# A hybrid mLSTM and delta-rule layer on one core: transposes, UL copies, sums and filler pieces of the delta rule placed differently

## The chip, the cores and the metric

The kernel runs on one core of a Trainium2 chip. The metric is the device time of one execution in microseconds. Several executions were timed, and the time of a kernel is their median. A profile is of one single execution, with a time of its own. Engines are named as in the profile: PE is TensorE (matmuls; PEld its weight loads), DVE is VectorE, ACT is ScalarE, POOL is GpSimd, SP is the engine whose queue issues most loads from memory.

## The reference

One layer, 256 tokens, model width 2048, fp32. Two recurrent branches read the same normalised input; each is projected, gated and merged, then a SwiGLU feed-forward part (FFN) follows.

```python
mod = c_act @ ada_w + ada_b                      # six vectors of 2048: shift, scale, gate, twice
h = rms_norm(x, norm_mix_w) * (1 + scale_m) + shift_m
proj = h @ w_in
(a_q, a_k, a_v, a_o, a_i, a_f, b_qkv, b_z, b_beta, b_a, merge) = jnp.split(proj, IN_SPLITS, axis=-1)
...
h_a = bidirectional(mlstm_chunkwise, (q_a, k_a, v_a), ...)          # 4 heads
y_a = (sigmoid(a_o) * rms_norm(h_a, mlstm_norm_w)) @ w_branch_a
qkv = silu(centred_depthwise_conv(b_qkv, gdn_conv_w))
...
o_b = bidirectional(gated_delta_chunkwise, (q_b, k_b, v_b), ...)    # 16 heads of 128
y_b = (rms_norm(o_b, gdn_norm_w) * silu(b_z)) @ w_branch_b
x = x + gate_m * ((g_a * y_a + g_b * y_b) @ w_out)
hf = rms_norm(x, norm_ffn_w) * (1 + scale_f) + shift_f
x = x + gate_f * ((silu(gt) * up) @ w_down)      # gt, up = split(hf @ w_gate_up)
```

The gated delta rule works in chunks of 64 tokens, forward and backward. Each chunk needs the inverse of a 64 x 64 unit triangular matrix:

```python
a_mat = eye(CHUNK) + betac[..., :, None] * einsum('nbhid,nbhjd->nbhij', kc, kc) * decay_strict
t_mat = triangular_solve(a_mat, eye(CHUNK), left_side=True, lower=True, unit_diagonal=True)
```

## The kernel before

Every projection is a matmul in which both sides are split into a high and a low part, three products each. The weights come from memory in chunks of 1 MB into `raw` (three buffers, loads issued on the SP queue). ScalarE copies half a chunk into `wh`, VectorE makes `wl` as the difference, and TensorE multiplies `wh` by the high part of the activation, `wh` by the low part, and `wl` by the high part. `wh` and `wl` have three buffers each. Half a chunk is one piece: twelve matmuls with 512 columns in `tjob` (lines 165, 166, 181 to 183), or 24 with 256 columns in `fjob` and in the jobs of the delta rule's own projections (lines 141, 142, 145 to 147; their tiles carry the letter b and the head, as in acc_b).

Jobs that nobody waits for soon are kept as a list of pieces, `fills`: `fill(n)` issues the next n of them, in the order z (the output gate of a group's heads), v, mb, o, a, ma and so on. They are put between the steps of the serial parts, so that TensorE has work while those steps wait for other engines. The total number of pieces is fixed; whatever is not used early is issued at the end of the stage by `fill(1000)`.

A second list, `background`, holds the sums of the modulation vectors (`ada_part` 2, 3 and 4, 17 items each): a 1 MB load into a `raw` buffer, then one VectorE instruction of line 110, which multiplies it by the conditioning row and accumulates. `pump()` is called at the end of every job or chunk and issues one sum at each `every[0]`-th call; at 0 there are none. `sums(n)` issues n at once.

The sixteen heads of the delta rule are worked in four groups of four, each group in two pairs:

- `gdn_phase1` of a head: convolution taps on VectorE (line 263, tile cv), SiLU on ScalarE (line 264: kq, vf), transposes of vf into vps (line 496), norms, the products ks (line 524), masks, and copies of blocks into cc on ScalarE (lines 553, 556). Blocks go to memory and come back packed as `uu` (line 548).
- `gdn_invert` of a group: a serial loop on VectorE over `uu`, 30 steps (lines 576 and below), that inverts the 32 x 32 diagonal blocks. Its first instruction, the memset of line 571, needs uu to have arrived. Between stretches of the loop one piece is issued.
- `gdn_blocks` of a group: the inverted blocks come back as `cg`; from it the tiles R, X (line 610, ScalarE) and UL (line 615, eight copies of 32 x 256 on ScalarE, four for i = 0 and four for i = 1).
- `gdn_phase2` of a pair, nine steps: p1 to p4 build the inverse from the blocks (lines 630 to 666, with mask products pt on VectorE), then pa, pb, pc (lines 676 to 688, with copies z on ScalarE, lines 680 and 681), po, a norm, and last the transposes px (line 713) and per head a copy `obt` on ScalarE (line 715) that goes to memory.

The driver runs the nine steps of a pair and puts pieces between them (the tuples `after` and `last`); the pieces are the projections of the next pair of heads, taken from `stream`, then filler. After the two pairs of a group it puts the next group's z job in front of the filler and runs the next inversion. Most of the heavier instructions pass through `order(...)`, and the program's scheduler decides the final place of the instructions in each engine's queue.

Behind the delta rule comes the mLSTM stage: loads of the branch results (`o_load`), loads in `mlstm(h)`, pieces in front of and between them. Then the branch projections yb and ya, the output projection with `wo` in four jobs (o0 to o3, each of four chunks, two pieces a chunk) that end in `residual` on VectorE, and the FFN.

Of the kernel before, what the change touches and what calls it, by code (L numbers as in the profile page):

```python
# [11 lines left out]
AF = mybir.ActivationFunctionType  # L12
# [40 lines left out]
def hybrid_block(ctx: ExitStack, tc: tile.TileContext, xr, nfr, crow, pk_d, cst_d, ada2, ada4, win0, winb, wint, wba, wbb, wo, wgu, wd, out, dbg=None):  # L53
    nc = tc.nc
    V, S, G, PE = nc.vector, nc.scalar, nc.gpsimd, nc.tensor
# [12 lines left out]
    def big(p, dt, name):  # L68
        return p.tile([P, KB, T], dt, tag="b16", name=name)

    def order(ins, yes=True):

        return tc.keep_in_program_order(ins) if yes else ins
# [43 lines left out]
    count, every = [0], [0]  # L117

    def sums(n=1):

        while n and background:
            if next(background[0], None):
                n -= 1
            else:
                background.pop(0)

    def pump():
        count[0] += 1
        if every[0] and count[0] % every[0] == 0:
            sums()  # L130
# [22 lines left out]
    def tjob(name, chunks, xh, xl, done, early=0):  # L153

        raws = {}

        def halves(u, k0):
            if u not in raws:  # L160
                raws[u] = st.tile([P, 4, 512], F32, tag="raw", bufs=3, name=f"raw_{name}_{u}")
                nc.sync.dma_start(raws[u], chunks[u])
            wh = st.tile([P, 2, 512], F32R, tag="wh", bufs=3, name=f"wh_{name}_{u}_{k0}")
            wl = st.tile([P, 2, 512], F32R, tag="wl", bufs=3, name=f"wl_{name}_{u}_{k0}")
            order(S.activation(wh, raws[u][:, k0 : k0 + 2], AF.Copy), early)  # L165
            order(V.tensor_tensor(wl, raws[u][:, k0 : k0 + 2], wh.bitcast(F32), ALU.subtract), early)  # L166
            return wh, wl

        todo = [(u, k0) for u in range(len(chunks)) for k0 in (0, 2)]
        made = [halves(*q) for q in todo[:early]]  # L170
        if early:
            yield True
        ps = [acc_ps.tile([P, 512], F32, tag="acc", name=f"acc_{name}_{t}") for t in range(2)]
        last = 4 * len(chunks) - 1
        for u, k0 in todo:
            wh, wl = made.pop(0) if made else halves(u, k0)
            for k in range(2):
                kk = 4 * u + k0 + k
                for t in range(2):
                    c = slice(t * P, (t + 1) * P)  # L180
                    PE.matmul(ps[t], xh[:, kk, c], wh[:, k], start=kk == 0, stop=False)  # L181
                    PE.matmul(ps[t], xl[:, kk, c], wh[:, k], start=False, stop=False)  # L182
                    PE.matmul(ps[t], xh[:, kk, c], wl[:, k], start=False, stop=kk == last)  # L183
            if k0:
                pump()
                if u == len(chunks) - 1:
                    done(ps)
            yield True

    def run(job):  # L190
        for _ in job:
            pass
# [3 lines left out]
    def fill(n=1):  # L196

        while n and fills:
            if next(fills[0], None):
                n -= 1  # L200
            else:
                fills.pop(0)
# [84 lines left out]
    def z_job(g, early=0):  # L287
        def done(ps):
            szs[g] = evp.tile([P, 2, 512], F32, tag="sz", bufs=1, name=f"sz{g}")
            for t in range(2):  # L290
                S.activation(szs[g][:, t], ps[t], AF.Silu)
        return tjob(f"z{g}", [wint[g, u] for u in range(4)], hh, hl, done, early)

    def b_job(h, j):
        return fjob(f"b{h}_{j}", winb[3 * (h - GRP) + j], lambda ps: gdn_conv(h, j, ps))
# [109 lines left out]
    with ExitStack() as s0:  # L405
# [29 lines left out]
        for b in range(KB):  # L435
# [6 lines left out]
            f = pk[:, PK_NMIX + b : PK_NMIX + b + 1]  # L442
# [29 lines left out]
    UL = bk.tile([P, 2, 8, P], F32, name="UL")  # L472
# [118 lines left out]
    def gdn_blocks(g):  # L591

        cg = bk.tile([P, 2, 512], F32, tag="uu", bufs=1, name=f"cg{g}")
        for b in range(4):
            G.dma_start(cg[32 * b : 32 * b + 32, 0], inv_d[g][:, b].rearrange("j x i -> j (x i)"))
        yield
        order(V.transpose(cg[:, 1], cg[:, 0]))
        F_, Bt, Ft, B_ = (cg[:, i // 2, (i % 2) * 256 : (i % 2 + 1) * 256].rearrange("p (m c) -> p m c", m=8) for i in range(4))

        def mix(dst, a, ca, b, cb):  # L600
            order(V.tensor_scalar(dst, b, cb, None, ALU.mult))
            order(V.scalar_tensor_tensor(dst, a, ca, dst, ALU.mult, ALU.add))

        mix(R[:, 0], Ft, even, Bt, odd)
        mix(R[:, 1], B_, even, F_, odd)
        yield
        for i, ab in enumerate(((Ft, Bt), (B_, F_))):
            for b in range(4):
                r = slice(32 * b, 32 * b + 32)
                order(S.activation(X[r, i, :, b % 2], ab[b // 2][r], AF.Copy))  # L610
            yield
        for i, a in enumerate((F_, B_)):
            for b in range(4):
                r = slice(32 * b, 32 * b + 32)
                order(S.activation(UL[r, i, :, r], a[r], AF.Copy))
            yield

    def gdn_phase2(g, p):
# [51 lines left out]
        r = bk.tile([P, 2, 2, P], F32, tag="r", bufs=1, name=f"r{g}_{p}")  # L670
# [34 lines left out]
        for e in range(2):  # L705
            h, hl_ = 4 * g + 2 * p + e, 2 * p + e
# [3 lines left out]
        for e, on in enumerate(ons):  # L710
            h, hl_ = 4 * g + 2 * p + e, 2 * p + e
            for t in range(2):
                PE.transpose(px[:, (2 * e + t) * P : (2 * e + t + 1) * P], on[:, t], ident)
            obt = bk.tile([P, T], F32, tag="obt", bufs=2, name=f"obt{h}")
            S.activation(obt, px[:, e * T : (e + 1) * T], AF.Copy, scale=pk[:, PK_GNW + h : PK_GNW + h + 1])
            S.dma_start(ob_d[g][hl_], obt)
# [33 lines left out]
    def stream(h0):  # L750

        todo = []

        def piece():

            for q in list(todo):
                q[0] -= 1
                if not q[0]:
                    todo.remove(q)
                    next(heads1[q[1]])  # L760

        for h in range(h0, min(h0 + 2, NH_B)):
            for j in range(3):
                for _ in b_job(h, j):
                    piece()
                    yield True
            todo += [[2, h], [4, h]]
        while todo:
            fill(1)
            piece()  # L770
            yield True
        while True:
            fill(1)
            yield True
# [16 lines left out]
    def invert(g):  # L791
        gen = gdn_invert(g)
        next(gen)
        fill(4)
        for _ in gen:
            fill(1)

    invert(0)
    for g in range(4):
        blocks = gdn_blocks(g)  # L800
        next(blocks)
        fill(8)
        next(blocks)
        fill(1)
        pairs = [gdn_phase2(g, p) for p in range(2)]
        every[0] = (0, 2, 2, 2)[g]
        for p in range(2):
            pieces = stream(4 * g + 2 * p + 4)
            for n in range(1, 10):
                next(pairs[p], None)  # L810
                if p == 0:
                    next(blocks, None)
                for _ in range(after[n] if g < 3 else last[n]):
                    next(pieces)
            for _ in pairs[p]:
                pass

            if g < 3:
                while 4 * g + 2 * p + 5 not in heads:
                    next(pieces)  # L820
        if g < 3:
            fills.insert(0, z_job(g + 1))
            every[0] = 0
            invert(g + 1)
# [138 lines left out]
    cores = steps(mlstm(0), mlstm(1))  # L963
    o4s = [o_load(g) for g in range(2)]
    every[0] = 0
    fill(2)
    next(cores)
    fill(6)
    for g in range(2):
        o_split(g, o4s[g])  # L970
        o4s.append(o_load(g + 2))
# [20 lines left out]
    mgh, mgl = big(bigC, F32R, "mgh"), big(bigC, F32R, "mgl")  # L992
# [10 lines left out]
    wp = pool(sw, "wp")  # L1003
# [14 lines left out]
    gm = wp.tile([P, D], F32, name="gm")  # L1018
    row(2, gm, wp)

    def residual(t, g, ps, gate, ss, rp):
        c = slice(g * 512, (g + 1) * 512)
        tm = rp.tile([P, 512], F32, tag="tm", bufs=2, name=f"tm{ss.name}_{t}_{g}")
        V.tensor_tensor(tm, ps, gate[:, c], ALU.mult)
        V.tensor_tensor(x1[:, t, c], x1[:, t, c], tm, ALU.add)
        S.activation(tm, x1[:, t, c], AF.Square, accum_out=ss[:, t, g : g + 1])
# [6 lines left out]
        return rs  # L1033

    ss1 = xp.tile([P, 2, 4], F32, name="ss1")
    for g in range(4):
        every[0] = 1 if g in (1, 2) else 2
        run(tjob(f"o{g}", [wo[g, u] for u in range(4)], mgh, mgl, lambda ps: [residual(t, g, ps[t], gm, ss1, wp) for t in range(2)]))
    if dbg is not None and "x1" in dbg:
        G.dma_start(dbg["x1"], x1)  # L1040
    sums(P)
# [15 lines left out]
    for q in range(4):  # L1057
# [3 lines left out]
        for e2 in range(2):  # L1061
            px = gps(f"pxn{q}_{e2}")
            hf = hp.tile([P, 2, T], F32, tag="hf", bufs=1, name=f"hf{q}_{e2}")
            for e in range(2):
                f = 2 * e2 + e
# [14 lines left out]
    for j in range(FB // 4):  # L1080
# [5 lines left out]
        for e2 in range(2):  # L1086
            px = gps(f"pxf{j}_{e2}")
            for e in range(2):
                f = 2 * e2 + e
# [122 lines left out]
```

## Time and profile before

| | us |
|---|---|
| median of 3 runs | 2104.58 |
| the runs | 2102.53 to 2105.44 |
| the profiled execution | 2102.55 |
| its span in the trace | 2100.8 |
| PE busy | 2034.4 |
| DVE busy | 1404.8 |
| ACT busy | 1042.3 |

The mean clock granted to TensorE was 0.986 of full speed. In the trace the delta rule's pairs run from about 314 to 977 us: group 0's pairs from 314 and 374, group 1's from 498 and 558, group 2's from 692 and 761, group 3's from 887, with the z jobs and inversions between them. The mLSTM stage and yb follow, the output projection runs from 1255 to 1336, and the FFN from there to the end.

How lines are read: in a list by time, a row gives start, duration, engine, line, operation, output <- inputs, shapes and count, and in brackets the idle time of the engine in front of it and what ended that wait. In a table of windows, a row gives the stretch, its length, then busy time and instruction count of each engine asked for, the granted clock (1.00 is full speed), the share of time that the DMA engines were busy, and GB/s. A group row gives busy time and mean ns of one, then the engine's idle time ahead of the group and what ended it.

### The profile page before, as it was taken

How to read it: one execution, taken by the hardware profiler on the slowest of the kernel's cores; microseconds unless marked ns; L12 is line 12 of the kernel's file. 1: busy time of each engine (PE TensorE's matmuls, PEld its weight loads, DVE VectorE, ACT ScalarE, POOL GpSimd, SP SyncE). 2: the span in 40 equal slices, each digit the busy share in tenths (PEclk: the TensorE clock that was granted, in tenths of full speed). 3: DMA queues.
4: the chain of work that ended last, by engine and by line, in shares of the span. 5: the costliest groups of instructions: out<-in, count | busy, mean ns of one | idle time of the engine just before them, and what ended most of it. 6: DMA issues, size and time to landing. Idle time of an engine off the chain costs nothing.

```text
span 2100.8 us, 26981 instructions
## 1 busy us (share of the span) xinstructions
PE 2034.4 (97%) x10374; PEld 1702.8 (81%) x10374; DVE 1404.8 (67%) x2065; ACT 1042.3 (50%) x1546; POOL 95.8 (5%) x189
## 2 busy tenths in 40 slices
PE   8999999999999999999999999899999999999997
PEld 6877789978988888889777877688888888878885
DVE  6787686787877687865677678765556554454544
ACT  2146548756774677565444443344444444444442
POOL 0002210110111011100000000000000000000000
PEclk9999999999999999999999999999999999999999
DMA  9986665566766565767886688566666765555553
GB/s 384 420 315 205 170 210 162 171 189 243 225 195 213 178 213 211 236 247 255 321 298 235 260 288 326 192 220 223 257 223 222 257 206 195 184 198 199 190 190 120
DMA packets 81971, 485.65 MB, mean 231 GB/s; under 512 B 10521, under 2 KB 20001, under 8 KB 27441
## 3 DMA queue, kind: packets, MB, share of 16 engines
q1 hardware_dynamic: 68672, 459.34, 60.9%
q0 software_dynamic: 5856, 9.49, 2.9%
q10 hardware_dynamic: 7314, 15.10, 1.9%
q8 instruction: 81, 1.33, 0.3%
q14 instruction: 48, 0.39, 0.1%
HBM read 467.07 MB, written 16.82 MB: 230 GB/s over the span
## 4 chain that ended last, share of the span: by engine, by line
PE 80%; DVE 7%; DMA 6%; ACT 4%; issue 2%; POOL 0%; SPq 0%; DVEq 0%; ACTq 0%; POOLq 0%
PE acc_gt L181 4%; PE acc_gt L182 4%; PE acc_up L181 4%; PE acc_up L182 4%; PE acc_d L181 4%; PE acc_up L183 4%; PE acc_d L182 4%; PE acc_d L183 4%; PE acc_gt L183 4%; PE first L452 3%; PE acc_b L147 2%; PE acc_b L145 2%; PE acc_b L146 2%; PE acc_o L183 2%; PE acc_o L181 2%; PE acc_o L182 2%
## 5 line engine op out<-in xcount | busy, mean ns | idle before, releaser
L166 DVE TENSOR_TENSOR wl_d<-raw_d,wh_d 128x1024 fp32r<-128x1024 f32 x88 | 107.9, 1226 | 123.2 <-ACT wh_d L165 123.2
L166 DVE TENSOR_TENSOR wl_up<-raw_up,wh_up 128x1024 fp32r<-128x1024 f32 x88 | 107.9, 1226 | 111.7 <-ACT wh_up L165 111.7
L145 PE MATMUL acc_b<-hh,wh_b 128*128 128x256 f32 x576 | 165.2, 287 | 4.7 <-ACT wh_b L141 4.7
L110 DVE SCALAR_TENSOR_TENSOR ada<-ada,crow 128x2048 f32<-128x2048 f32 x64 | 146.4, 2288 | 28.4 <-DMA ada<-ada 28.2
L166 DVE TENSOR_TENSOR wl_gt<-raw_gt,wh_gt 128x1024 fp32r<-128x1024 f32 x88 | 107.2, 1225 | 86.6 <-ACT wh_gt L165 86.6
L147 PE MATMUL acc_b<-hh,wl_b 128*128 128x256 f32 x576 | 162.3, 282 | 1.1 <-DVE wl_b L142 1.1
L165 ACT ACTIVATE wh_d<-raw_d 128x1024 fp32r<-128x1024 f32 x88 | 93.3, 1061 | 138.9 <-PE acc_d L182 134.0
L146 PE MATMUL acc_b<-hl,wh_b 128*128 128x256 f32 x576 | 161.2, 280 | 0.0
L165 ACT ACTIVATE wh_gt<-raw_gt 128x1024 fp32r<-128x1024 f32 x88 | 93.3, 1060 | 133.9 <-PE acc_gt L182 73.4
L165 ACT ACTIVATE wh_up<-raw_up 128x1024 fp32r<-128x1024 f32 x88 | 93.3, 1060 | 117.8 <-PE acc_up L182 82.5
L181 PE MATMUL acc_gt<-wh_gt,hfh 128*128 128x512 f32 x352 | 138.8, 397 | 2.7 <-ACT hfh L205 2.4
L182 PE MATMUL acc_gt<-wh_gt,hfl 128*128 128x512 f32 x352 | 139.4, 396 | 0.0
L183 PE MATMUL acc_gt<-wl_gt,hfh 128*128 128x512 f32 x352 | 138.6, 394 | 0.0
L181 PE MATMUL acc_d<-wh_d,ffh 128*128 128x512 f32 x352 | 137.5, 391 | 0.0
L182 PE MATMUL acc_d<-wh_d,ffl 128*128 128x512 f32 x352 | 137.4, 390 | 0.0
L183 PE MATMUL acc_d<-wl_d,ffh 128*128 128x512 f32 x352 | 137.0, 389 | 0.0
L183 PE MATMUL acc_up<-wl_up,hfh 128*128 128x512 f32 x352 | 136.9, 389 | 0.0
L181 PE MATMUL acc_up<-wh_up,hfh 128*128 128x512 f32 x352 | 136.9, 389 | 0.0
L182 PE MATMUL acc_up<-wh_up,hfl 128*128 128x512 f32 x352 | 136.9, 389 | 0.0
L452 PE MATMUL first<-x,raw 128*128 128x256 f32 x512 | 115.1, 387 | 6.7 <-ACT x L446 6.7
L452 PEld LDWEIGHTS first<-x,raw 128*128 128x128 f32 x512 | 98.7, 194 | 23.0 <-ACT x L446 9.3
L145 PEld LDWEIGHTS acc_b<-hh,wh_b 128*128 128x128 f32 x576 | 110.2, 191 | 5.1 <-ACT wh_b L141 5.1
(345 smaller groups left out, 5256.8 us busy)
## 6 DMA issues: line engine op xcount, KB each, us to landing
ada<-ada SPq DMA_DIRECT2D x64, 1024.0 KB, 5.0
raw_gt<-wgu SPq DMA_DIRECT2D x44, 1024.0 KB, 5.0
raw_up<-wgu SPq DMA_DIRECT2D x44, 1024.0 KB, 4.9
raw_d<-wd SPq DMA_DIRECT2D x44, 1024.0 KB, 4.9
raw_b<-winb SPq DMA_DIRECT2D x36, 1024.0 KB, 5.1
ra<-ada SPq DMA_DIRECT2D x32, 1025.0 KB, 14.6
raw<-win SPq DMA_DIRECT2D x16, 1024.0 KB, 12.8
raw_z<-wint SPq DMA_DIRECT2D x16, 1024.0 KB, 4.9
```

The lines of the kernel that those rows point to most:

```text
L110: V.scalar_tensor_tensor(raw, raw, 1.0, row_c[:, :D], ALU.mult, ALU.mult, accum_out=mod[:, c0 + b : c0 + b + 1])
L145: PE.matmul(o, wh[:, k], hh[:, kk], start=kk == 0, stop=False)
L146: PE.matmul(o, wh[:, k], hl[:, kk], start=False, stop=False)
L147: PE.matmul(o, wl[:, k], hh[:, kk], start=False, stop=kk == KB - 1)
L165: order(S.activation(wh, raws[u][:, k0 : k0 + 2], AF.Copy), early)
L166: order(V.tensor_tensor(wl, raws[u][:, k0 : k0 + 2], wh.bitcast(F32), ALU.subtract), early)
L181: PE.matmul(ps[t], xh[:, kk, c], wh[:, k], start=kk == 0, stop=False)
L182: PE.matmul(ps[t], xl[:, kk, c], wh[:, k], start=False, stop=False)
L183: PE.matmul(ps[t], xh[:, kk, c], wl[:, k], start=False, stop=kk == last)
L452: PE.matmul(first[o], raw[:, o], x[:, b], start=b == 0 and o % 2 == 0, stop=b == KB - 1 and o % 2 == 1)
```

## The change

Six edits in the order of work; what is computed, and the number of loads and of matmuls, stay the same.

1. Of the eight UL copies of a group, the four with i = 1 run on VectorE.
2. In the last step of a pair, the transposes of both heads are issued before the two obt copies.
3. Ahead of the first inversion six filler pieces are issued, not four. The other inversions keep four.
4. In groups 1 to 3 the sums are off in the first pair and one per job in the second; before, it was one per two jobs in both.
5. In the mLSTM stage the pieces before and after the branch's own loads are four and four, not two and six.
6. In the output projection the sums stand at fixed pieces of each job, three per job; before, they went by `pump()`, every chunk in the middle jobs and every second chunk in the outer ones. There are twelve in both.

```diff
@@ -612,7 +612,10 @@
         for i, a in enumerate((F_, B_)):
             for b in range(4):
                 r = slice(32 * b, 32 * b + 32)
-                order(S.activation(UL[r, i, :, r], a[r], AF.Copy))
+                if i:
+                    order(V.tensor_copy(UL[r, i, :, r], a[r]))
+                else:
+                    order(S.activation(UL[r, i, :, r], a[r], AF.Copy))
             yield
@@ -711,6 +714,8 @@
             h, hl_ = 4 * g + 2 * p + e, 2 * p + e
             for t in range(2):
                 PE.transpose(px[:, (2 * e + t) * P : (2 * e + t + 1) * P], on[:, t], ident)
+        for e in range(2):
+            h, hl_ = 4 * g + 2 * p + e, 2 * p + e
             obt = bk.tile([P, T], F32, tag="obt", bufs=2, name=f"obt{h}")
             S.activation(obt, px[:, e * T : (e + 1) * T], AF.Copy, scale=pk[:, PK_GNW + h : PK_GNW + h + 1])
             S.dma_start(ob_d[g][hl_], obt)
@@ -791,7 +796,7 @@
         gen = gdn_invert(g)
         next(gen)
-        fill(4)
+        fill(4 if g else 6)
@@ -803,8 +808,8 @@
         pairs = [gdn_phase2(g, p) for p in range(2)]
-        every[0] = (0, 2, 2, 2)[g]
         for p in range(2):
+            every[0] = p if g else 0
             pieces = stream(4 * g + 2 * p + 4)
@@ -963,9 +968,9 @@
     every[0] = 0
-    fill(2)
+    fill(4)
     next(cores)
-    fill(6)
+    fill(4)
@@ -1033,9 +1038,12 @@
     ss1 = xp.tile([P, 2, 4], F32, name="ss1")
+    every[0] = 0
     for g in range(4):
-        every[0] = 1 if g in (1, 2) else 2
-        run(tjob(f"o{g}", [wo[g, u] for u in range(4)], mgh, mgl, lambda ps: [residual(t, g, ps[t], gm, ss1, wp) for t in range(2)]))
+        job = tjob(f"o{g}", [wo[g, u] for u in range(4)], mgh, mgl, lambda ps: [residual(t, g, ps[t], gm, ss1, wp) for t in range(2)])
+        for i, _ in enumerate(job):
+            if i in ((2, 4, 6) if g < 3 else (1, 2, 4)):
+                sums()
```

## The prediction

> **What bounds the kernel now.** I read the head of the page first, then the chain that ended last, then the stages one by one.
>
> ```profile
> span 2100.8 us, 26981 instructions
> PE 2034.4 (97%) x10374; PEld 1702.8 (81%) x10374; DVE 1404.8 (67%) x2065; ACT 1042.3 (50%) x1546; POOL 95.8 (5%) x189
> PE 80%; DVE 7%; DMA 6%; ACT 4%; issue 2%; POOL 0%; SPq 0%; DVEq 0%; ACTq 0%; POOLq 0%
> ```
>
> TensorE is busy for 97% of the span, and the chain runs through it for 80%. The matmuls stay the same in number, so this change can win only TensorE's pauses and what a pause costs behind itself. The second part is seen in TensorE's windows (length, busy time, granted clock):
>
> ```profile
> 261.53:264.94 3.41, 1.53 (x7) 1.00 0.26 40
> 264.94:268.35 3.41, 3.41 (x10) 0.50 0.65 271
> 667.20:688.90 21.70, 21.70 (x96) 1.00 0.68 230
> 701.85:705.26 3.41, 1.23 (x12) 1.00 0.00 0
> 705.26:708.67 3.41, 3.41 (x19) 0.50 0.47 111
> 715.50:718.91 3.41, 1.43 (x13) 1.00 1.01 406
> 718.91:725.74 6.83, 5.79 (x25) 0.50 0.50 180
> 1312.70:1316.11 3.41, 1.73 (x8) 1.00 0.56 221
> ```
>
> A stretch of 3.41 us with 1.53, 1.23 or 1.43 busy is followed by one or two such stretches at a clock of 0.50; the stretch with 1.73 busy is not (no half clock follows at 1316). So a pause of about 1.9 us that falls into one stretch costs another 1.7 us (half of 3.41), and a pause of 1.7 us does not. The third row prices a piece of filler: 96 matmuls in 21.70 us, so 12 of them take 2.7 us.
>
> The stages that the change touches, all engines (length; busy of PE, PEld, DVE, ACT, POOL; clock): the two pairs of group 0, both pairs of group 1, both pairs of group 2, the output projection.
>
> ```profile
> 314.00:374.00 60.00, 59.11 (x459) 55.26 (x458) 40.60 (x84) 48.95 (x96) 3.57 (x7) 1.00 0.49 156
> 374.00:433.00 59.00, 59.00 (x461) 55.59 (x460) 45.74 (x96) 45.30 (x91) 7.01 (x14) 1.00 0.56 166
> 498.00:558.00 60.00, 58.86 (x445) 54.35 (x444) 48.56 (x91) 47.54 (x94) 3.56 (x7) 1.00 0.68 220
> 558.40:622.60 64.20, 60.37 (x477) 56.42 (x475) 54.12 (x116) 49.06 (x100) 8.12 (x16) 1.00 0.68 220
> 692.00:761.00 69.00, 63.80 (x447) 58.98 (x446) 46.57 (x88) 46.09 (x93) 3.56 (x7) 0.93 0.56 190
> 761.00:822.00 61.00, 59.94 (x446) 55.53 (x445) 51.24 (x104) 45.16 (x91) 5.38 (x10) 1.00 0.64 224
> 1254.80:1335.80 81.00, 77.85 (x333) 61.42 (x331) 61.84 (x61) 31.99 (x41) 0.00 (x0) 1.00 0.79 297
> ```
>
> Group 0 runs its two pairs without sums in 60 and 59 us; group 2's first pair, with sums, takes 69. That is the largest loss in the reach of the change.
>
> **The change part by part.** The sum goes against the profiled execution's 2102.55 us; the median of the runs shown is 2.03 above it.
>
> *Six pieces ahead of the first inversion.*
>
> ```profile
> 254.57 1.20 DVE L166 TENSOR_TENSOR wl_v<-raw_v,wh_v 128x1024 fp32r<-128x1024 f32 x1
> 261.31 0.09 DVE L571 MEMSET uu<- 64x32 f32 x1
> 262.14 1.21 DVE L166 TENSOR_TENSOR wl_v<-raw_v,wh_v 128x1024 fp32r<-128x1024 f32 x1
> 263.40 0.51 PE L183 MATMUL acc_v<-wl_v,hh 128*128 128x512 f32 x1 [1.93 <-DVE wl_v L166]
> ```
>
> The fifth weight subtraction stands in VectorE's queue behind the memset of L571, which waits until 261.3 for the packed blocks to come by DMA; TensorE waits 1.93 for it. With six pieces ahead, two more subtractions stand before the memset. At one per 2.7 us the sixth is done about 254.6 + 5.4 + 1.2 = 261.2, as the memset becomes ready, so the inversion is not late, and the next subtraction is due 5.4 us later than now. The pause (1.93) and its half-clock stretch (1.7) go: +3.6. At worst the wait moves to the seventh subtraction: 0.
>
> By the Trainium skill ("TensorE: Matmul & The Clock Gate", Part 1: The HAM clock gate), the clock drops after at least one idle window of about 3.4 us. By that alone, pauses of 1.93 and 2.19 us would cost only themselves, and the sum below would be smaller by some 6.3 us. The rows disagree: stretches that were still busy for 1.53 and 1.23 us of 3.41 halved it, so I give that reading no chance of its own.
>
> *Half of the UL copies on VectorE.*
>
> ```profile
> L615 ACT ACTIVATE UL<-cg x32: 399/413/418, 324.0 to 903.2; 32x256 f32<-32x256 f32 x32
> L666 DVE COPY UL<-p x8: 427/428/428, 332.3 to 950.4; 64x256 f32<-64x256 f32 x8
> L110 DVE SCALAR_TENSOR_TENSOR ada<-ada,crow x4: 2268/2284/2293, 557.5 to 603.7; 128x2048 f32<-128x2048 f32 x4
> ```
>
> Each group takes 4 × 0.413 = 1.65 us off ScalarE. No row shows this copy on VectorE; the nearest is L666 with the same 256 columns at 0.428, read from PSUM, which I take: 1.7 us more VectorE work per group, between 0.8 (half of it, as both ends are now in SBUF) and 1.7. The first pairs have VectorE at 40.60 to 48.56 of 60, so this lies under TensorE; where that cover is gone it costs 1.7 a group. What it frees is in group 1's first pair: of its 60.00 − 58.86 = 1.14 idle, a UL copy ends nearly all. I take half, +0.5 (0 to 1.1). In group 0 the new TensorE order leaves just two matmuls between the first two block products, so one more wait of the size of that stage's present idle (60.00 − 59.11 = 0.9) is due: −0.7 (−0.9 to 0).
>
> *No sums in the first pairs.* This bears on group 2.
>
> ```profile
> 702.09 1.69 ACT L615 ACTIVATE UL<-cg 32x256 f32<-32x256 f32 x4
> 704.90 0.38 PE L145 MATMUL acc_b<-hh,wh_b 128*128 128x256 f32 x1 [2.19 <-ACT wh_b L141]
> 713.37 2.29 DVE L110 SCALAR_TENSOR_TENSOR ada<-ada,crow 128x2048 f32<-128x2048 f32 x1
> 717.13 0.42 ACT L264 ACTIVATE kq<-cv 128x256 f32<-128x256 f32 x1 [3.91 <-DVE cv L263]
> 719.48 0.58 PE L145 MATMUL acc_b<-hh,wh_b 128*128 128x256 f32 x1 [2.55 <-ACT wh_b L141]
> ```
>
> The first pause is a weight copy queued behind four UL copies (702.09), late because the raw buffer before it came late. The second starts with a sum: at 713.37 it holds VectorE for 2.29 us, the convolution behind it ends late, ScalarE sits 3.91 us in front of kq, and the weight copy behind kq holds TensorE for 2.55. Without sums neither the 2.29 us nor the 1 MB transfers through the three shared raw buffers stand there. The stage's loss is 69.00 − 63.80 = 5.2 idle, and (3.41 + 5.79)/2 = 4.6 at half clock: 9.8. I keep 0.5 as what group 0's first pair shows to remain: +9.3 (5 to 9.8).
>
> *Sums in the second pairs, one per job, and both heads' transposes together.*
>
> ```profile
> 618.01 0.38 PE L713 MATMUL px<-cst,on 128*128 128x128 f32 x2
> 621.63 0.47 ACT L715 ACTIVATE obt<-px,pk 128x256 f32<-128x256 f32 x1
> 622.16 0.44 PE L713 MATMUL px<-cst,on 128*128 128x128 f32 x2 [3.77 <-ACT obt L715]
> 623.10 0.61 PE L181 MATMUL acc_z<-wh_z,hh 128*128 128x512 f32 x1 [0.50 <-ACT wh_z L165]
> ```
>
> In group 1 the second head's transposes wait 3.77 for the first head's copy, which stands on ScalarE behind the cc copies of head 11; then the z job waits 0.50, and a half-clock stretch follows (1.7). In the new order the four transposes run on end, and three z weight copies stand ahead of the cc and obt copies on ScalarE: 3.77 + 0.50 + 1.7 = 6.0 goes. Against it VectorE gets eight sums for four: 54.12 + 4 × 2.3 = 63.3 in a stage of 64.2 that is to become 60. That doesn't fit quite; some of the dec and mask work spills into the z job behind it, where only inversions queue. I take 1.0 off: +5.0 (−1 to 6).
>
> In group 2's second pair the new order is worse at the end.
>
> ```profile
> 801.86 0.38 ACT L681 ACTIVATE z<-pc,sm 128x128 f32<-128x128 f32 x1
> 815.85 1.28 ACT L264 ACT_TABLE_LOAD   x1
> 817.15 0.42 ACT L264 ACTIVATE vf<-cv 128x256 f32<-128x256 f32 x1
> 818.08 0.38 PE L496 MATMUL vps<-cst,vf 128*128 128x128 f32 x2
> 818.88 0.60 ACT L276 ACTIVATE ev_mb<-acc_mb 128x512 f32<-128x512 f32 x1
> ```
>
> Before, 37 filler matmuls (8.4 us) stand between head 15's last projection and vps of L496. In the new order only one piece (2.7 us) does, and ScalarE must first evict that piece's sum (0.60), load a table and take the root for the other head (1.28), load another (1.28) and make vf (0.42); vf to vps is 0.5. So TensorE idles about 4.1 us, bounded by 0 and by 8.4 − 2.7 = 5.7. Also po now follows pc with no filler between, and waits the four z copies, 1.1 us (three steps of 0.25 and the last's 0.38). One half-clock stretch is sure with that much idle: 1.7. Now the stage loses 61.00 − 59.94 = 1.06, of which 0.9 goes: −(4.1 + 1.1 + 1.7) + 0.9 = −6.0 (−9.5 with two stretches, to +0.9).
>
> *mLSTM, fill 4 and 4.*
>
> ```profile
> L181 PE MATMUL acc_ma<-wh_ma,hh 128*128 128x512 f32 x128 | 51.2, 400 | 4.1 <-ACT wh_ma L165 4.1
> ```
>
> That wait is a weight transfer queued on SP behind the branch's own loads. SP's queue still has those loads in front of a weight chunk, one chunk later: 0 (−2 to +3, as 4.1 may shrink, or gain a half stretch).
>
> *Output projection.* Sums at fixed pieces, three per four chunks. It idles 81.00 − 77.85 = 3.15 now, mostly for subtractions behind the residuals and sums. One of them is freed, another moves behind four residual operations: +0.7 (−1.5 to 2). The FFN's instructions are the same.
>
> Sum: 3.6 + 0.5 − 0.7 + 9.3 + 5.0 − 6.0 + 0 + 0.7 = 12.4 us. 2102.55 − 12.4 = 2090.15, and with the 2.03 to the median **2092.2 us**. Its own range is 2087 to 2098.
>
> **The rivals.**
>
> *A, slower: VectorE saturates in the second pairs.* Sums run there one per job, and 63.3 of some 60 us is over the brim. If a sum strikes as the one at 713.37 did, each strike costs 2.55 + half of 5.79 = 5.4. Two in each second pair of groups 1 and 2 make 21.8: 2092.2 + 21.8 = 2114. It decides from three strikes on (16.3 above 12.4). For it: the load, and the three raw buffers that sums and weights share. Against it: group 1's second pair had four sums and no such pause, and group 2's had 61.00 with as many.
>
> *B, the end of group 2 doesn't stall.* If vf is ready when TensorE gets there, the −6.0 becomes +0.9: 2085.3. For it: now vf is queued behind two weight copies, 1.06 each, which stand after it in the new order. Against it: two table loads must pass after the mb eviction.
>
> *C, a repair only moves its wait.* If the inversion's pause shows up one piece later, 3.6 is lost: 2095.8; if group 1's second pair gives its 5.0 back to late dec and mask work (54.12 grows to 63.3): 2097.2. For it: both have VectorE in order behind them.
>
> **How the numbers follow.** Forecast 0.40, C 0.20, A 0.17, B 0.15, and 0.08 for a mixture of A and C that comes out near the old time. 0.2% of the time, 4.2 us, is about what a measurement of this kernel can tell from no change. Forecast, B and C lie below 2100.4: 0.75 faster; the mixture gives 0.08 same; A gives 0.17 slower. The range reaches from B with group 1 and the projection at their best (2085.3 − 1.0 − 1.3 = 2083) to the mixture's end, 2106; most of A is left out.
>
> **What would show it.** Right: no half clock near 264.94, 623.34, 705.26 and 718.91; group 2's first pair about 60 us long; px with no idle before it in group 1; a new pause of about 4 us before vps of head 15, with a half-clock stretch behind it; a pause of about 4 us still in front of an ma weight. Wrong: waits of TensorE for wl_b or wh_b in the second pairs with L110 just ahead on VectorE (A); a wl_v pause near 267 (C); no vps pause (B).

## The result and the profile after

The changed kernel is slower: median 2117.01 us (2112.81 to 2117.84) against 2103.56 us for the kernel before, measured together. The ratio is 1.0053, with a 95% interval of 1.0033 to 1.0073. The prediction said 2092.2. The profiled execution took 2117.84 us.

Head of the page of the changed kernel, in the order of the one shown for before:

```profile
span 2116.1 us, 26986 instructions
PE 2038.0 (96%) x10374; PEld 1705.1 (81%) x10374; DVE 1408.3 (67%) x2081; ACT 1037.3 (49%) x1530; POOL 96.0 (5%) x189
PE 78%; DVE 9%; DMA 6%; ACT 4%; issue 2%; ACTq 0%; DVEq 0%; SPq 0%; POOL 0%; POOLq 0%
```

TensorE's work is the same, so the stages are best compared by what each loses: TensorE's idle time plus half of its busy time at half clock. The table is worked out in this way from the matmul rows and the clock of each trace (one execution each, us). Stages begin at the matmuls of p1 and z, behind group 3's last pair, at the matmuls of y_a and at the FFN's first transposes. The two columns on the right belong to experiments below.

| lost in | before | changed | edit 3 alone | all but edit 4 |
|---|---|---|---|---|
| start, with the first inversion | 28.3 | 23.7 | 23.1 | 24.3 |
| group 0, both pairs | 0.9 | 6.7 | 6.8 | 6.7 |
| next inversion, group 1 first pair | 1.8 | 2.6 | 1.5 | 2.5 |
| group 1 second pair, z and inversion | 8.5 | 6.8 | 1.2 | 4.8 |
| group 2 first pair | 9.8 | 5.7 | 2.0 | 0.7 |
| group 2 second pair | 1.1 | 14.0 | 0.8 | 6.8 |
| z, inversion and both pairs, group 3 | 0.1 | 0.0 | 5.0 | 3.2 |
| mLSTM, y_b | 7.2 | 8.7 | 7.8 | 9.6 |
| y_a, output projection | 7.5 | 14.0 | 8.7 | 9.5 |
| FFN | 21.3 | 20.2 | 21.3 | 21.6 |
| sum | 86.4 | 102.3 | 78.1 | 89.6 |

The sums differ by 15.9 us between the first two columns, the spans by 15.3: the account is nearly whole. Two rows carry most of it, group 2's second pair (12.9) and the output projection (6.5); group 0 loses 5.8 more as well, and other rows gain. A row is firm to some 3 us only: the run with edit 6 undone (below) has the same instructions in the same order up to the output projection, and there its idle times are within 1 us of the changed kernel's in each stage of the delta rule, but its half-clock share is 0 in group 0 in place of 3.4, and 4.5 in group 2's second pair in place of 2.9.

The stages of the changed kernel (length; busy of PE, PEld, DVE, ACT, POOL; clock): group 0's second pair, both pairs of group 1, both of group 2. Below them VectorE's time in the sums of line 110 alone, for the four pairs of groups 1 and 2 (two instructions a sum).

```profile
375.80:439.30 63.50, 62.02 (x445) 57.66 (x444) 46.97 (x97) 45.85 (x90) 7.08 (x14) 0.95 0.52 152
505.30:565.20 59.90, 59.01 (x446) 54.71 (x445) 45.22 (x91) 47.81 (x94) 3.56 (x7) 1.00 0.52 167
565.60:626.50 60.90, 59.13 (x494) 56.66 (x493) 57.33 (x110) 43.83 (x90) 7.08 (x14) 1.00 0.80 272
696.40:761.70 65.30, 61.33 (x445) 55.93 (x444) 43.84 (x90) 45.93 (x90) 3.56 (x7) 0.97 0.50 158
762.20:837.20 75.00, 63.92 (x446) 56.72 (x445) 61.77 (x118) 49.57 (x100) 7.54 (x14) 0.95 0.60 217
```

```profile
505.30:565.20 59.90, 2.30 (x2) 1.00 0.52 167
565.60:626.50 60.90, 16.07 (x14) 1.00 0.80 272
696.40:761.70 65.30, 2.30 (x2) 0.97 0.50 158
762.20:837.20 75.00, 16.05 (x14) 0.95 0.60 217
```

Seven sums run in each second pair, as meant, but one runs in each first pair too, where `every` is 0. Group 2's first pair shows what that one does (rows in order of time):

```profile
743.85 0.33 SPq L109 DMA_DIRECT2D ada<-ada  x1
747.80 1.05 ACT L165 ACTIVATE wh_mb<-raw_mb 128x1024 fp32r<-128x1024 f32 x1
752.40 2.29 DVE L110 SCALAR_TENSOR_TENSOR ada<-ada,crow 128x2048 f32<-128x2048 f32 x1 [5.43 <-DMA ada<-ada]
754.69 1.22 DVE L166 TENSOR_TENSOR wl_mb<-raw_mb,wh_mb 128x1024 fp32r<-128x1024 f32 x1
755.96 0.50 PE L183 MATMUL acc_mb<-wl_mb,hh 128*128 128x512 f32 x1 [3.09 <-DVE wl_mb L166]
```

The sum belongs to the second pair's first job, and the scheduler placed it on VectorE ahead of a weight subtraction. VectorE then sits 5.43 us in front of it until its load has landed. The subtraction, whose ScalarE half was done at 748.85, runs only at 754.69, and TensorE waits 3.09. The end of group 2's second pair, on ScalarE and then TensorE:

```profile
817.96 1.28 ACT L276 ACT_TABLE_LOAD   x1
819.25 0.60 ACT L276 ACTIVATE ev_mb<-acc_mb 128x512 f32<-128x512 f32 x1
819.87 1.28 ACT L733 ACT_TABLE_LOAD   x1
821.48 1.28 ACT L264 ACT_TABLE_LOAD   x1
822.77 0.42 ACT L264 ACTIVATE vf<-cv 128x256 f32<-128x256 f32 x1
823.24 0.69 PE L496 MATMUL vps<-cst,vf 128*128 128x128 f32 x2 [5.78 <-ACT vf L264]
```

This is the stall that was predicted: the mb eviction, two table loads and vf, one behind the other, with one piece of filler. A third table load stands ahead of the eviction. Earlier in the same pair a sum holds VectorE while it waits for its load, and a copy of p into UL behind it (line 669, not one of those of edit 1) makes TensorE wait; the matching copy on ScalarE had run at 777.61.

```profile
778.62 2.29 DVE L110 SCALAR_TENSOR_TENSOR ada<-ada,crow 128x2048 f32<-128x2048 f32 x1 [2.23 <-DMA ada<-ada]
781.35 0.43 DVE L669 COPY UL<-p 64x256 f32<-64x256 f32 x1
781.84 0.49 PE L680 MATMUL pa<-vv,UL 128*128 128x128 f32 x2 [1.81 <-DVE UL L669]
```

TensorE's windows around the stalls (length, busy, clock):

```profile
258.00:268.00 10.00, 10.00 (x45) 1.00 0.71 221
375.10:378.51 3.41, 2.03 (x14) 1.00 0.23 77
378.51:385.34 6.83, 6.73 (x31) 0.50 0.37 124
753.98:757.39 3.41, 1.43 (x6) 1.00 0.46 144
757.39:760.80 3.41, 3.41 (x7) 0.50 0.62 199
822.24:829.07 6.83, 5.83 (x15) 0.50 0.68 211
```

The pause at the first inversion is gone (first row), and so is the wait of px in group 1: four transposes and then z without a break.

```profile
626.52 0.60 PE L716 MATMUL px<-cst,on 128*128 128x128 f32 x4
626.87 0.48 PE L181 MATMUL acc_z<-wh_z,hh 128*128 128x512 f32 x1
```

In group 0 a new pause of 1.48 us brings two half-clock stretches (378.51): the mask product pt stands on VectorE behind the masks of a phase-1 head.

```profile
377.54 0.44 DVE L539 STREAM_TRANSPOSE mi<-mb 128x256 f32<-128x256 f32 x1
377.90 0.66 DVE L634 TENSOR_TENSOR pt<-p,cst 128x512 f32<-128x512 f32 x1
378.61 1.70 PE L642 MATMUL p<-R,pt 128*128 128x32 f32 x7 [1.48 <-DVE pt L634]
```

In the output projection a sum waits for its load with subtractions behind it again, and later subtractions stand behind the four residual operations:

```profile
1261.45 2.29 DVE L110 SCALAR_TENSOR_TENSOR ada<-ada,crow 128x2048 f32<-128x2048 f32 x1 [2.94 <-DMA ada<-ada]
1263.67 3.49 DVE L166 TENSOR_TENSOR wl_o<-raw_o,wh_o 128x1024 fp32r<-128x1024 f32 x3
1264.95 0.74 PE L183 MATMUL acc_o<-wl_o,mgh 128*128 128x512 f32 x2 [2.67 <-DVE wl_o L166]
1303.04 1.28 DVE L1030 TENSOR_TENSOR x<-x,tmss 128x512 f32<-128x512 f32 x2
1305.51 0.73 PE L183 MATMUL acc_o<-wl_o,mgh 128*128 128x512 f32 x2 [2.21 <-DVE wl_o L166]
```

### The profile page after: what moved, and what is told of

The parts are those of the page before. It is cut to its first block, busy times and chain, and to the rows that moved or that the text cites. A ratio compares the mean times of both kernels' runs of the same rounds, so it can differ in the third digit from the quotient of the medians.

```text
span 2116.1 us, 26986 instructions
## 1 busy us (share of the span) xinstructions
PE 2038.0 (96%) x10374; PEld 1705.1 (81%) x10374; DVE 1408.3 (67%) x2081; ACT 1037.3 (49%) x1530; POOL 96.0 (5%) x189
## 4 chain that ended last, share of the span: by engine, by line
PE 78%; DVE 9%; DMA 6%; ACT 4%; issue 2%; ACTq 0%; DVEq 0%; SPq 0%; POOL 0%; POOLq 0%
PE acc_gt L181 4%; PE acc_gt L182 4%; PE acc_up L183 4%; PE acc_up L182 4%; PE acc_d L182 4%; PE acc_d L181 4%; PE acc_up L181 4%; PE acc_gt L183 4%; PE acc_d L183 4%; PE first L452 3%; PE acc_o L183 2%; PE acc_o L181 2%; PE acc_o L182 2%; DMA ada<-ada 2%; PE acc_b L145 2%
## 5 line engine op out<-in xcount | busy, mean ns | idle before, releaser
L110 DVE SCALAR_TENSOR_TENSOR ada<-ada,crow 128x2048 f32<-128x2048 f32 x64 | 146.4, 2287 | 30.5 <-DMA ada<-ada 30.5
L147 PEld LDWEIGHTS acc_b<-hh,wl_b 128*128 128x128 f32 x576 | 109.4, 190 | 5.4 <-DVE wl_b L142 5.4
```

Source lines behind the costliest of these rows:

```text
L110: V.scalar_tensor_tensor(raw, raw, 1.0, row_c[:, :D], ALU.mult, ALU.mult, accum_out=mod[:, c0 + b : c0 + b + 1])
L147: PE.matmul(o, wl[:, k], hh[:, kk], start=False, stop=kk == KB - 1)
```

## The experiments

Theory Q: the sums cost the time, as edits 4 and 6 place them in VectorE's queue. Rival O: the moved UL copies and transposes upset the order, and the sums are incidental. All ratios are to the kernel before on the same chip; the changed kernel is 1.0053.

### Edits undone one at a time

Edit 4 undone:

```diff
         for p in range(2):
-            every[0] = p if g else 0
+            every[0] = (0, 2, 2, 2)[g]
```

> The change without edit 4 (sums again one per two jobs in both pairs of groups 1 to 3). Theory Q, sums at the head of VectorE's queue cost the time: group 2's second pair, which lost 14.0 us to idle and half clock in the changed kernel, falls to 5 or less and the median comes to 2103 to 2110. Rival O, the moved UL copies and transposes upset the order and the sums are incidental: the loss of that stage stays above 9 and the median above 2113.

Measured 0.9971 (0.9953 to 0.9989): 17 us off the changed kernel, more than the whole loss. Group 2's second pair fell to 6.8, not to 5.

Edit 6 undone (`every[0] = 1 if g in (1, 2) else 2` and the plain `run` again):

> The change without edit 6 (output projection pumps its sums as before). Theory Q: the waits of 2.67 and 2.21 us for wl_o behind sums and their half-clock stretches go, ya and the output projection lose about 7.5 us in place of 14.0, median about 2110.5. Rival O: those waits come from work that earlier edits pushed back, so at least half of the 6.5 us stays and the median is 2114 or more.

Measured 1.0033 (1.0015 to 1.0051), 4 us faster, though the interval overlaps that of the changed kernel. Its share of the stage (14.0 to 7.8) is as theory Q had it.

Edit 1 undone:

```diff
-                if i:
-                    order(V.tensor_copy(UL[r, i, :, r], a[r]))
-                else:
-                    order(S.activation(UL[r, i, :, r], a[r], AF.Copy))
+                order(S.activation(UL[r, i, :, r], a[r], AF.Copy))
```

> The change without edit 1 (all UL copies on ScalarE). Theory Q: within 2 us of the changed kernel, 2115 to 2119, with the two stalls of group 2's second pair (pa behind a sum, vps) still there. Rival O: the waits for pt and UL in groups 0 and 2 go, 4 to 8 us faster, 2109 to 2113.

Measured 1.0051 (1.0035 to 1.0067): the UL copies make no difference that can be measured.

Edit 2 undone (the two lines `for e in range(2):` and `h, hl_ = ...` ahead of obt removed):

> The change without edit 2 (each head's copy straight after its transposes). Theory Q: edit 2 is a gain of its own, so without it the time is the same or up to 5 us longer, 2117 to 2122, and px waits again for obt. Rival O: 3 to 6 us faster, 2111 to 2114, as the stall before the second block product of group 0 (1.48 us and two half-clock stretches) goes.

Measured 1.0026 (1.0011 to 1.0042), 6 us faster by the two ratios, whose intervals overlap a little. This is the size that rival O had, but not its place: group 0 still lost 6.5 us there, and px waited 2.53 for obt again.

### Fewer edits together

Edits 4 and 6 undone:

> The change without edits 4 and 6 (the sums as before everywhere). Theory Q: both undone edits add up, some 17 and 4 us off the changed kernel, 2094 to 2099 where the kernel before has 2104 to 2106. Rival O: the order that the other edits make costs as much as it brings, 2101 or more.

Measured 0.9951 (0.9932 to 0.9970). As far as the intervals tell, the two add up.

Edits 2, 4 and 6 undone:

> The change without edits 2, 4 and 6 (left are the UL copies, the six pieces and the mLSTM pieces). If edit 2 is a loss in itself, as the run without it alone suggests (some 5 us faster than the changed kernel), this is 3 to 6 us faster than the run without edits 4 and 6. If edit 2 only met the sums badly, it is the same within 2 us or up to 5 us slower, with px waiting for obt again.

Measured 0.9952 (0.9933 to 0.9970): without the sums' new places, edit 2 makes no difference. If it cost anything above, that was an encounter with them.

Edit 3 alone on the kernel before:

```diff
-        fill(4)
+        fill(4 if g else 6)
```

> The kernel before with edit 3 alone (six pieces ahead of the first inversion). As predicted: the wl_v pause of 1.93 us and the half-clock stretch at 264.9 go, 3.6 us faster, 0.998 of the kernel before, and group 0's second pair keeps its loss of 0. Rival: the two pieces used early are missing later, group 0's second pair loses 3 to 5 us as in the changed kernel, and the time is the same as before within 1.5 us.

Measured 0.9941 (0.9927 to 0.9956), 12 us faster, the lowest median of the study (2091.75 us against 2103.49), level within the intervals with the change without edits 4 and 6. Both expectations missed: group 0 does lose as in the changed kernel, and yet the gain is three times the predicted one. Its windows for group 1's second pair and both pairs of group 2:

```profile
563.90:623.50 59.60, 59.60 (x498) 57.51 (x496) 50.81 (x103) 44.69 (x91) 7.07 (x14) 1.00 0.67 222
688.60:750.00 61.40, 59.39 (x447) 54.61 (x445) 47.06 (x88) 45.98 (x93) 3.57 (x7) 1.00 0.62 213
750.00:811.20 61.20, 60.41 (x450) 55.46 (x451) 53.17 (x110) 46.42 (x95) 5.37 (x10) 1.00 0.65 227
```

The px stall of group 1 and the 9.8 us of group 2's first pair, which the prediction gave to edits 2 and 4, go with edit 3 alone, with sums in both pairs.

Eight pieces instead of six, on the kernel before (`fill(4 if g else 8)`):

> The kernel before with eight pieces ahead of the first inversion. If the gain of edit 3 alone (12 us) comes from the removed pause and from all that follows being issued two pieces earlier, as a rule of the count, eight gives 10 us or more too, 0.995 or less, unless the inversion becomes late itself. If it comes from how just this order of pieces happens to fall against the later waits, eight gives only the removed pause, about 4 us, 0.998, or less.

Measured 0.9981 (0.9963 to 0.9999). So the gain isn't a rule of the count: some 4 us, the size of the removed pause, remain, and the other 8 us of six pieces go with how just that order falls.

Edit 2 alone on the kernel before:

> The kernel before with edit 2 alone. As predicted for it: the wait of px for obt in group 1 (3.77 us, 0.50 behind it and 1.7 at half clock) goes and little else moves, 4 to 6 us faster, 0.997 to 0.998 of the kernel before. Rival: edit 2 brings nothing of its own (the stall goes as soon as the order of pieces shifts), 0.999 to 1.002.

Measured 1.0001 (0.9985 to 1.0017). The transposes run on end, and the wait moves one step on, to the z weights:

```profile
616.76 0.60 PE L713 MATMUL px<-cst,on 128*128 128x128 f32 x4
623.04 0.79 PE L181 MATMUL acc_z<-wh_z,hh 128*128 128x512 f32 x1 [5.69 <-ACT wh_z L165]
```

Edit 4 alone on the kernel before:

> The kernel before with edit 4 alone. As predicted for it: group 2's first pair loses under 2 us in place of 9.8, and group 2's second pair some 7 in place of 1.1, together 2 to 4 us faster, 0.998 to 0.999. If edit 4 costs by itself: 1.002 or more, with the wait for vf and waits for wl_b and wh_b in the second pairs.

Measured 1.0054 (1.0035 to 1.0073): by itself edit 4 costs as much as the whole change. In group 2's first pair the same early sum as above:

```profile
749.58 2.29 DVE L110 SCALAR_TENSOR_TENSOR ada<-ada,crow 128x2048 f32<-128x2048 f32 x1 [5.80 <-DMA ada<-ada]
751.87 1.22 DVE L166 TENSOR_TENSOR wl_mb<-raw_mb,wh_mb 128x1024 fp32r<-128x1024 f32 x1
753.15 0.80 PE L183 MATMUL acc_mb<-wl_mb,hh 128*128 128x512 f32 x1 [3.66 <-DVE wl_mb L166]
```

Edits 3 and 4 together:

> The kernel before with edits 3 and 4. If edit 4 costs by itself: 10 us or more slower than edit 3 alone, 1.000 of the kernel before or more, with one piece (12 matmuls) between head 15's last projection and vps and a wait for vf there. If it costs only together with the other edits: within 4 us of edit 3 alone, 0.994 to 0.996.

Measured 1.0027 (1.0014 to 1.0040), against 0.9941 for edit 3 alone: 18 us. The wait for vf is there again, 5.78 us. Edit 4 costs without the other edits.

### What in a sum costs

Half of each sum's work, on the changed kernel (the second half of the columns is left out of the sum; in this run and the others here the scheduler may order other instructions anew too):

```diff
-            V.scalar_tensor_tensor(raw, raw, 1.0, row_c[:, :D], ...
+            V.scalar_tensor_tensor(raw[:, :1024], raw[:, :1024], 1.0, row_c[:, :1024], ...
```

> The changed kernel with each sum taken over the first 1024 of 2048 columns only (the second half is left out), its 1 MB load whole. VectorE has 1.1 us less work per sum and waits for the same load. Theory Qa (what costs is the wait for the load at the head of VectorE's queue): the wait for wl_mb at the end of group 2's first pair stays at 1.9 us or more, and the median falls by less than 6 us, to 2111 or more. Theory Qb (what costs is VectorE's own work in the second pairs): the loss of group 2's second pair falls from 14.0 to 7 or less and the median by 8 us or more, to 2109 or less.

Measured 0.9986 (0.9977 to 0.9996), 14 us faster. The stages fit theory Qb in part only: the wait for wl_mb stays (2.50), group 2's second pair keeps 12.4 of its 14.0, and most of the gain lies in the z job behind group 1 (4.7) and in the output projection (5.6). In the second pair the idle time does fall, from 11.1 to 7.2, with the wait for vf down from 5.78 to 3.25; more half clock (5.1 for 2.9) hides it. The wait ahead of the early sum is as long as before:

```profile
748.38 1.22 DVE L110 SCALAR_TENSOR_TENSOR ada<-ada,crow 128x1024 f32<-128x1024 f32 x1 [5.71 <-DMA ada<-ada]
750.87 0.79 PE L183 MATMUL acc_mb<-wl_mb,hh 128*128 128x512 f32 x1 [2.50 <-DVE wl_mb L166]
```

Half of each load, the work kept (the sum is taken twice over the same 1024 columns, by a second instruction that this excerpt doesn't show):

```diff
-            nc.sync.dma_start(raw, ada4[part - 2, b])
+            nc.sync.dma_start(raw[:, :1024], ada4[part - 2, b][:, :1024])
```

> The changed kernel with 512 KB loaded per sum in place of 1 MB, and the sum taken twice over the same 1024 columns (the other columns are left out). VectorE's work per sum is the same within 0.2 us, the load half. Theory Qa: the wait for wl_mb in group 2's first pair falls below 1.5 us and that for wl_o in the output projection's first job goes, the median falls by 8 us or more, to 2109 or less. Theory Qb: by less than 4 us, to 2113 or more.

Measured 1.0033 (1.0019 to 1.0047), 4 us faster, with overlapping intervals; group 2's second pair loses 14.3, of which 8.3 is idle. Neither reading holds alone, and half the load brings little.

Sums held in program order, `order(V.scalar_tensor_tensor(...))`:

> The changed kernel with every sum held at its place in program order on VectorE, so that the scheduler can't put it ahead of weight subtractions that were issued earlier. If the early placing is what costs (the sum at 752.40 waited 5.43 us for its load with wl_mb behind it), the wait for wl_mb in group 2's first pair and that for wl_o in the first output job fall below 1.5 us, and the median falls by 5 us or more, to 2112 or less. If it is the number of sums in a pair whatever their place, it stays at 2114 or more.

Measured 1.0048 (1.0033 to 1.0063). The two waits named go: group 2's first pair loses 0.9 in place of 5.7, the projection 8.5 in place of 14.0. But group 2's second pair loses 17.2 (11.2 of it idle, as in the changed kernel), and the total hardly moves. Early placing is a cause in those two stages and not in the largest.

No sums in group 2:

```diff
-            every[0] = p if g else 0
+            every[0] = p if g in (1, 3) else 0
```

> The changed kernel with the sums off in both pairs of group 2 as well; they are made up for later, in the stages behind. Theory Q: group 2's first pair loses under 2 us in place of 5.7 (no early-placed sum holds wl_mb) and its second pair under 6 in place of 14.0; the median falls by 8 us or more, to 2109 or less, unless the later stages pay. Rival O: the second pair keeps its wait of some 5.8 us for vf, which stands behind table loads and the mb eviction on ScalarE, and its loss stays above 9.

Measured 1.0051 (1.0031 to 1.0072), yet both pairs of group 2 run nearly without loss:

```profile
694.10:754.40 60.30, 59.41 (x449) 55.07 (x448) 42.29 (x86) 45.83 (x90) 3.56 (x7) 1.00 0.49 153
754.50:814.50 60.00, 59.72 (x450) 54.66 (x448) 42.96 (x99) 47.73 (x94) 5.37 (x10) 1.00 0.45 153
```

The later stages pay it back: the sums left over run at the end of the output projection, between the residuals and ahead of the FFN's first scaling (VectorE):

```profile
1338.13 0.69 DVE L1030 TENSOR_TENSOR x<-x,tmss 128x512 f32<-128x512 f32 x1
1338.74 0.68 DVE L1029 TENSOR_TENSOR tmss<-acc_o,gm 128x512 f32<-128x512 f32 x1
1339.34 2.28 DVE L110 SCALAR_TENSOR_TENSOR ada<-ada,crow 128x2048 f32<-128x2048 f32 x1
```

y_a and the projection lose 21.0 and the FFN 29.0, together 16 more than in the changed kernel.

No sums in groups 1 and 2, one per job in group 3 and one per chunk in y_b, with edits 1, 3 and 5:

> The kernel before with edits 1, 3 and 5, no sums at all in groups 1 and 2, one per job in group 3 and one per chunk in the y_b stage. Theory Q: the four pairs of groups 1 and 2 lose under 6 us together in place of 16.3 in the kernel before; if group 3 and the branch projections have room for the sums, the median is 0.990 to 0.996 of the kernel before. Rival: the sums cost as much where they go, 0.998 or more.

Measured 1.0000 (0.9986 to 1.0015). The four pairs lose 3.4 in place of 16.3, but y_b loses 7.9 in place of 1.0, and group 3's pairs with the mLSTM stage 10.1 in place of 6.2. The same edits with the sums as before measured 0.9952 above, so this way of moving the sums costs some 10 us.

Small sums, with and without a buffer of their own (192 columns, taken six times; the other columns are left out; the excerpt shows the buffer and the load of the first):

```diff
-            raw = st.tile([P, D], F32, tag="raw", bufs=3, ...
-            nc.sync.dma_start(raw, ada4[part - 2, b])
+            raw = st.tile([P, 192], F32, tag="ada", bufs=1, ...
+            nc.sync.dma_start(raw, ada4[part - 2, b][:, :192])
```

> The changed kernel with sums over 192 of 2048 columns, taken six times (VectorE's work per sum about 2.2 us as before; the other columns are left out), and the 192 columns loaded into a buffer of their own, so that the sums take none of the three raw buffers. If the shared buffers cause the loss of group 2's second pair: it falls from 14.0 to under 6 there, and the median by 6 us or more, to 2111 or less. If VectorE's work or ScalarE's order causes it: above 9 stays.

> The same small sums, six times 192 columns, with their small load still into a raw buffer. If the shared buffers cause the loss of group 2's second pair: 10 us or more stay there, and the run is 5 us or more slower than the one with a buffer of its own. If the size of the load is what costs: under 6 here as well, and the two runs are the same within 3 us.

Measured 1.0072 (1.0046 to 1.0098) and 0.9979 (0.9960 to 0.9998). On the buffers the pair is inconclusive: with a buffer of their own all but a few sums ran before group 2's second pair, which then had none. VectorE in the sums in that pair, first with the own buffer, then with the shared one:

```profile
790.30:850.50 60.20, 0.00 (x0) 1.00 0.47 161
```

```profile
756.40:829.90 73.50, 15.04 (x84) 0.93 0.43 143
```

The second still loses 12.7 us in that pair (7.6 idle, with a wait of 3.0 for vf), with a load of less than a tenth and VectorE's work kept. So the size of the load is at most a part of the cost there. Elsewhere it counts: the run is some 15 us faster than the changed kernel, 6.5 of them in y_a and the projection and 3.1 in group 2's first pair, the two stages where a sum was seen to wait for its load.

## Why the prediction was wrong

**What failed first is the attribution.** The prediction took each pause of the kernel before, named the edit that works on its cause, and added. That holds only where the instruction order around the pause stays. Two filler pieces issued earlier shifted the whole order, and edit 3 alone removed what the forecast gave to edits 2 and 4: the px stall and what followed it (8.5 us lost in group 1's second pair, z job and inversion, 1.2 left) and 9.8 in group 2's first pair (2.0 left). To edit 4 the forecast gave a gain, and it is the loss: without edits 4 and 6 the change gains 10 us (0.9951), edit 4 put back costs 17 (1.0033), and edit 6 another 4 (1.0053).

**First inversion, +3.6.** Right. The pause and its half-clock stretch are gone, 28.3 − 23.7 = 4.6 with the noise of the start in it; eight pieces give a gain of that size too.

**UL copies, +0.5 and −0.7.** The copies themselves don't matter. One took 0.284 us on VectorE, in the bounds (0.2 to 0.43), and group 1's first pair idles 0.9 for 1.1. Group 0's −0.7 was mis-sized: −5.8, of which 2.4 is idle and 3.4 half clock that doesn't come in every execution. With edit 3 alone it is the same, so it belongs to the shifted order.

**No sums in the first pairs, +9.3.** Wrong. The step read `every` = 0 as no sum in that pair; the trace has one there, placed early and waiting for its load. The stage gained 4.1.

**Second pairs, +5.0 and −6.0.** In group 1 the gain was 1.7; TensorE waited 2.9 us for a z subtraction behind the start of the next inversion and 1.4 for a weight subtraction behind a sum of line 110; the forecast had neither. In group 2 the vf stall was the right step and place: 5.78 us for 4.1, as the forecast left out the third table load (1.28). The wait for the z copies was 0.5 for 1.1. What was missing beside them are waits for UL and weights, 4.4 us in the middle of the pair, 1.81 of them behind the sum at 778.62, and more half clock (2.9 for 1.7). Together −12.9, outside the term's own bound, which its parts put at −9.3 and not at −9.5.

**mLSTM, 0.** Right: the ma wait stayed (3.83 for 4.11) and that stage with y_b moved by 1.5. No run undoes edit 5 alone.

**Output projection, +0.7.** Wrong in sign: −6.5. One wait for wl_o (2.67) stands behind a sum that waits for its load, which the term did not have. The other (2.21) stands behind the four residual operations, which the term named and counted as small. A half-clock stretch follows each. Undoing edit 6 gives back 4 us of the time.

**Rival A** had the sign and nearly the time (2114). That edit 4's sums are the cause is shown: they cost 17 us undone, 18 added to edit 3 and 11 added alone. A's sign of being right is there too, small: waits of 1.4 us for wl_b in group 1's second pair and of 0.7 in group 2's, with L110 just ahead on VectorE. But the two strikes in each second pair that made its 21.8 did not come: group 1's gained 1.7 and group 2's lost 12.9, and the rest of the way came from terms that A took over from the forecast. So the near time is luck. VectorE's time in the sums is a part of the largest stage only, as half of it leaves 7.2 of 11.1 us idle.

Nine kernels here have the vf stall (3.0 to 5.8 us). All nine have edit 4's sums in that pair, and 12 filler matmuls stand between head 15's last projection and vps; in the kernels without the stall, 24 or 37 do. The way from one to the other takes 5.8 to 8.5 us in the first kind and 8.0 to 8.5 in the second (11.7 with edit 4 alone, which has the sums and 24 matmuls, and where a wait of 3.6 for an mb weight lies in it). So this part goes with the sums and with the order of instructions that the scheduler then makes; which of the two makes the stall isn't shown. Whether the shared raw buffers make the other waits of that pair stays open.

Rivals B and C did not come: vps does wait, and TensorE is busy throughout from 258 to 268.

## What to carry to other kernels

Background work on an in-order engine costs what stands behind it: its own time, and also the wait for its load, which shows as idle time of that engine in front of it while the next instruction's data is already there. Where a scheduler places instructions, look at the trace for work in a stage that the source doesn't issue there, and measure each edit alone before adding up terms; a shift of two filler pieces was worth more here than all the repairs aimed at. Moving such sums elsewhere needs a stage with room on that engine: both tries here paid the gain in the pairs back later.

## What was not expected of the hardware

The busy share of a 3.41 us stretch doesn't decide alone whether the clock halves: the stretch at 375.10 was busy for 2.03 us and two half-clock stretches followed, where before one with 1.73 busy was followed by full clock. A 1 MB load for a sum, issued at 743.85, let its sum start only at 752.40, 8.6 us later, where the median of all 64 such loads from issue to landing is 5.0.
